# One matmul of 512 columns for two of 256 in the first half's dense products, operand tiles that stay allocated, and a three-chunk input projection

## The chip, the core and the metric

The kernel runs on one core of a Trainium2 chip. The metric is the device time of one execution in microseconds. The core has five engines that run side by side: TensorE (PE in the profile, with its weight loads as PEld), VectorE (DVE), ScalarE (ACT), GpSimd (POOL) and SyncE (SP, which only issues DMAs). TensorE's clock is granted at one of two levels, 2.4 GHz (shown as 1.0) or 1.2 GHz (0.5).

## The reference

One inference step of a trunk of two layers over T = 1088 tokens: a prompt of 1024 and eight samples of 8. All is float32. Cut to its frame:

```python
for layer in range(2):
    h = rmsnorm(x, norm_mix[layer])
    if layer == 0:
        u, q, k, v, b, a, z = split(h @ ab_w_in)          # 1024 -> 2568
        mix = concat([s5_mixer(u) with its GLU, gated_delta(q, k, v, b, a, z)]) @ ab_w_out
    else:
        r, k, v, decay, a, g = projections of h and of h shifted by a token
        y = rwkv7_scan(r, decay, k, v, a, ...)            # state 64 x 64, 16 heads, sequential in time
        mix = (norm(y) * g) @ w_o
    x = x + mix
    h = rmsnorm(x, norm_ffn[layer])
    x = x + (silu(h @ w_gate) * (h @ w_up)) @ w_down      # 1024 -> 2816 -> 1024
y = rmsnorm(x)
```

The final states of all recurrences are outputs too.

## The kernel before

Features lie on partitions (8 tiles of 128), tokens on columns. The tokens are worked in two halves (`HALF`, line 23): the first has 512 tokens in two chunks of 256, the second 576 in two chunks of 288. The order of the program is: the input projection, S5 and the first half of the gated-delta heads (`layer0`); then for each half the output projection (`project`, products `po`), the feed-forward net (`ffn`) and layer 1's projections (`RWKV.projections`, products `pj`); then for each half layer 1's output projection and feed-forward net.

A dense product (`mm`, L296) is exact to more than the matmul's own format: weight and operand are each split into a high and a low part, and for each of 8 contraction tiles there are three matmuls (high by high, high by low, low by high) into one bank of PSUM, each with its own weight load of 128 columns. A product of a whole column tile is so 24 matmuls. Each of the two chunks has its own products, one after the other, with the same weights. In the net, `pg` are the products of gate and up, `pd` those of down, which go in groups of three tiles of the hidden features (9 matmuls each). PSUM has two banks for all of these (`pa`), used in turn; VectorE empties a `pd` or `po` bank with one add into the residual stream (L508, L420), ScalarE and VectorE a `pg` bank with a tanh and products (L484 to L493). The weights come by SP's queue, are rounded on ScalarE (L284) and their low parts made on GpSimd (L285) or VectorE.

The operands' parts are tiles of one chunk each, `hi` and `lo`, taken anew for each use from rings of 16 (`hilo`, L392). The input projection (`pi`) takes all 1088 tokens in four chunks of 272 (`NCH`).

The recurrence of layer 1 (`RWKV.unit`, L1506 to L1687) goes by feature tile (8) and by segment (4 of 256 tokens, the last with the 64 sample tokens besides): 32 units. Each unit prepares its operands, inverts its triangular matrices (`inverse`, with a chain of 15 pairs of small VectorE products, L170 and L172), and then takes its 4 chunks of 64 tokens one after the other. One such step is a chain over TensorE and VectorE: L1636 (matmul into `pc`), L1638 (VectorE copy to `X`), L1640, L1642, L1644, L1647, and L1649, which leaves the state `H` for the next step. Results go to DRAM (`dyr`), and from there into layer 1's output projection. The units of the first half's segments run beside the second half's layer 0, those of the second half's segments beside the first half's layer 1.

What stands where on each engine is decided by a scheduler before the program runs: it lists the instructions by its own estimate of when each could go, and every engine then runs its list strictly in order. Nothing is moved at run time.

Of the kernel before, what the change touches and what calls it, by code (L numbers as in the profile page):

```python
# [31 lines left out]
class Fine:  # L32
    """Functions on small float32 tiles by DVE arithmetic, to float32's accuracy."""
# [42 lines left out]
    def log1p(self, out, e):  # L76
        """ln(1 + e) for e in [0, 1]."""
# [13 lines left out]
class Kern:  # L91
    def __init__(self, ctx, tc):
# [7 lines left out]
        # identity and the matrices of the norms' sums  # L100
# [14 lines left out]
        # block masks: row blocks of 16 and of 8, and which half of 32 a row is in  # L115
# [18 lines left out]
        # unit matrices of 16 in a lane's row  # L134
# [50 lines left out]
        # blocks of 32  # L185
# [24 lines left out]
        # blocks of 64  # L210
# [32 lines left out]
        # blocks of 128  # L243
# [31 lines left out]
    def weight(self, src, kt=8, m=128, tag="w", bufs=3, lo=None):  # L275
        """Loads [128, kt, m] and returns its high and low parts."""
# [67 lines left out]
    def spread(self, r):  # L344
        """stats()' result on all partitions."""
# [31 lines left out]
    def after(self, ins, n):  # L377
        """To be issued, on its engine, after the n-th of ins from their end."""
# [13 lines left out]
    def hilo(self, n=8):  # L392
        """Tiles of a chunk for the high and the low parts of n feature tiles."""
        return tuple([self.dp.tile([128, self.width], F32R, tag=t, name=t, bufs=16) for i in range(n)]
                     for t in ("hi", "lo"))
# [16 lines left out]
    def project(self, x, ys, chunks, w, ahead, n=8):  # L412
# [1650 lines left out]
```

## Time and profile before

| | us |
|---|---|
| median of 3 runs | 3808.33 (3807.59 to 3809.31) |
| the profiled execution's span | 3788.5 |
| PE busy | 3497.6 |
| DVE busy | 2510.2 |
| ACT busy | 1321.9 |
| POOL busy | 1321.9 |

The span goes from the first instruction to the last; the time of a run also has what lies around it, 19.8 us by these numbers. A busy PE is not a PE at its peak: the end of a matmul is modelled, and matmuls overlap. How long one matmul holds the engine is therefore read from how many start in a stretch in which nothing else ran, not from its mean duration.

### The profile page before, as it was taken

What the parts mean: (1) busy time and instruction counts of PE and PEld (TensorE: products, weight loads), DVE (VectorE), ACT (ScalarE), POOL (GpSimd) and SP (SyncE); (2) the same over time, 40 slices, a digit from 0 to 9 for tenths busy, and PEclk for the clock granted to TensorE, in tenths of its full rate; (3) what the DMA queues carried; (4) which work ended last, traced back from release to release, by engine and by line L of the source; (5) the groups of instructions that cost most, each with busy time, mean ns of one, the idle gap of its engine ahead of it and who ended that gap; (6) DMA issues with size and microseconds to landing.
All of it is one profiled execution on the core that took longest, in us unless ns stands there. A gap on an engine that the chain in (4) does not pass through costs nothing. (4 is left out here: it accounts for less than half of the span.)

```text
span 3788.5 us, 78549 instructions
## 1 busy us (share of the span) xinstructions
PE 3497.6 (92%) x30678; PEld 3214.4 (85%) x30678; DVE 2510.2 (66%) x6901; ACT 1321.9 (35%) x2944; POOL 1321.9 (35%) x1211
## 2 busy tenths in 40 slices
PE   7899998999988989999999889999999999899998
PEld 6889887999978877888888777888888888799997
DVE  7976878754466367777877574567788886553444
ACT  3333333222234443333333244433333333232222
POOL 3322233222235443333333264533333433332221
PEclk9989998999988999999999988998999999899999
DMA  3334442322223542122222224621222222312222
GB/s 104 93 88 124 104 126 70 93 88 95 93 73 102 184 147 70 58 78 82 87 76 73 80 73 140 210 82 54 81 88 92 90 75 82 126 64 81 88 78 69
DMA packets 331410, 356.44 MB, mean 94 GB/s; under 512 B 133272, under 2 KB 273304, under 8 KB 331040
## 3 DMA queue, kind: packets, MB, share of 16 engines
q1 hardware_dynamic: 321824, 342.52, 29.5%
q10 hardware_dynamic: 9216, 8.92, 0.7%
q8 instruction: 241, 3.95, 0.4%
q14 instruction: 129, 1.06, 0.1%
HBM read 285.34 MB, written 64.81 MB: 92 GB/s over the span
## 5 line engine op out<-in xcount | busy, mean ns | idle before, releaser
L285 POOL TENSOR_TENSOR wl<-raw,wh 128x1024 fp32r<-128x1024 f32 (+2 forms) x301 | 701.9, 2335 | 1095.7 <-ACT wh L284 1019.8
L296 PE MATMUL pg<-hi,wh 128*128 128x288 f32 (+1 forms) x2816 | 839.9, 298 | 18.8 <-DVE s L485 13.4
L296 PE MATMUL pg<-lo,wh 128*128 128x288 f32 (+1 forms) x2816 | 838.3, 298 | 6.8 <-DVE lo L383 5.0
L296 PE MATMUL pg<-hi,wl 128*128 128x288 f32 (+1 forms) x2816 | 836.8, 297 | 0.0
L296 PEld LDWEIGHTS pg<-hi,wh 128*128 128x128 f32 x2816 | 545.0, 194 | 31.3 <-DVE s L485 16.0
L296 PEld LDWEIGHTS pg<-lo,wh 128*128 128x128 f32 x2816 | 544.3, 193 | 18.1 <-DVE lo L383 7.0
L296 PEld LDWEIGHTS pg<-hi,wl 128*128 128x128 f32 x2816 | 544.7, 193 | 7.4 <-issue 1.6
L284 ACT CAST wh<-raw 128x1024 fp32r<-128x1024 f32 (+3 forms) x309 | 312.7, 1013 | 378.3 <-PE pg L296 103.9
L296 PE MATMUL pd<-ah,wdh 128*128 128x256 f32 (+1 forms) x1280 | 387.7, 303 | 20.9 <-DVE x L508 17.7
L296 PE MATMUL pd<-ah,wdl 128*128 128x256 f32 (+1 forms) x1280 | 370.7, 290 | 0.3 <-POOL wdl L285 0.3
L296 PE MATMUL pd<-al,wdh 128*128 128x256 f32 (+1 forms) x1280 | 370.7, 290 | 0.0
L296 PEld LDWEIGHTS pd<-ah,wdh 128*128 128x128 f32 x1280 | 241.9, 189 | 36.3 <-DVE x L508 21.2
L296 PE MATMUL pj<-lo,wh 128*128 128x256 f32 (+1 forms) x768 | 244.0, 318 | 17.5 <-DVE lo L383 14.5
L296 PE MATMUL pj<-hi,wh 128*128 128x256 f32 (+1 forms) x768 | 242.5, 318 | 15.7 <-ACT st L1371 7.2
L296 PEld LDWEIGHTS pd<-ah,wdl 128*128 128x128 f32 x1280 | 242.3, 189 | 1.7 <-POOL wdl L285 0.9
L296 PEld LDWEIGHTS pd<-al,wdh 128*128 128x128 f32 x1280 | 242.5, 189 | 0.8
L296 PE MATMUL pj<-hi,wl 128*128 128x256 f32 (+1 forms) x768 | 238.7, 313 | 0.4 <-POOL wl L285 0.2
L508 DVE TENSOR_TENSOR x<-x,pd 128x256 f32<-128x256 f32 (+1 forms) x384 | 162.4, 424 | 75.0 <-PE pd L296 70.7
L284 ACT CAST wdh<-raw 128x384 fp32r<-128x384 f32 (+1 forms) x224 | 111.2, 496 | 284.9 <-PE pd L296 196.8
L170 DVE TENSOR_TENSOR Tm<-L,T 32x15 f32<-32x15 f32 (+8 forms) x600 | 185.8, 310 | 29.5 <-DMA L<-dA 17.3
L172 DVE TENSOR_TENSOR T<-T,Tm 32x15 f32<-32x15 f32 (+8 forms) x600 | 184.6, 308 | 13.0
L296 PE MATMUL pi<-hi,wh 128*128 128x272 f32 x640 | 192.5, 301 | 0.2 <-ACT rows L1803 0.2
(639 smaller groups left out, 8199.9 us busy)
## 6 DMA issues: line engine op xcount, KB each, us to landing
raw<-in_wg SPq DMA_DIRECT2D x88, 512.0 KB
raw<-in_wup SPq DMA_DIRECT2D x88, 512.0 KB
raw<-in_wd SPq DMA_DIRECT2D x192, 192.0 KB
raw<-in_win SPq DMA_DIRECT2D x20, 512.0 KB
raw<-pr ACTq DMA_DIRECT2D x64, 136.0 KB
raw<-in_wk SPq DMA_DIRECT2D x16, 512.0 KB
raw<-in_wr SPq DMA_DIRECT2D x16, 512.0 KB
raw<-in_wv SPq DMA_DIRECT2D x16, 512.0 KB
```

Source lines behind the costliest of these rows:

```text
L170: v.tensor_mul(mm, L[:nl, j:j + 1, j + 1:16].to_broadcast([nl, j + 1, n]), T[:nl, 0:j + 1, j:j + 1].to_broadcast([nl, j + 1, n]))
L172: v.tensor_tensor(T[:nl, 0:j + 1, j + 1:16], T[:nl, 0:j + 1, j + 1:16], mm, op=op)
L284: nc.scalar.copy(wh, raw)
L285: (lo or nc.gpsimd).tensor_sub(wl, raw, wh)
L296: self.nc.tensor.matmul(ps, a[k], b[:, c:c + cn], start=i == 0, stop=i == last)
L508: v.tensor_add(x[m][:, c:c + cn], x[m][:, c:c + cn], ps)
```

## The change

Three things, in one diff.

1. `operands()` allocates the eight `hi` and eight `lo` tiles once, each with both chunks side by side ([128, 2, 288]); `part(i, ...)` gives the view of chunk i, `part(None, ...)` that of both as one operand of 2 x 256 columns. `hilo` and the lists of tiles that were handed around are gone.
2. In the first half (512 tokens), most dense products go over both chunks at once: one matmul of 512 columns into a whole PSUM bank where two of 256 stood. These are: gate and up of hidden tiles 2 to 21, down of all groups but the last (whose 8 output tiles still go chunk by chunk, as the norm of the next stage starts with the first chunk), in both layers; the S5 linear unit; layer 0's output projection but for its last contraction tile; tiles 0 to 5 of layer 1's output projection; keys 2 to 5, and receptances and values 1 to 5. The gate's bank is then emptied chunk by chunk (`yielded`), down's by one add of 512 columns. The second half (576 tokens, over the 512 of a bank) stays as it was.
3. The input projection takes three chunks (368, 360, 360) in place of four of 272, except for the rows and tiles that go with the norm at the very start.

```diff
+TCH = [(0, 368), (368, 360), (728, 360)]
+WIDE = 512
...
+    def operands(self):
+        self.H = tuple([self.dp.tile([128, 2, self.width], F32R, name="%s%d" % (t, k)) for k in range(8)]
+                       for t in ("hi", "lo"))
+    def part(self, i, cn, ks=range(8)):
+        return tuple([t[k][:, :, :cn] if i is None else t[k][:, i, :cn] for k in ks] for t in self.H)
...
-    def mm(self, ps, w, x, cn, c=0):
-        his, los = x
+    def mm(self, ps, w, x, cn=None, c=0):
+        his, los = x if cn is None else [[t[:, c:c + cn] for t in y] for y in x]
+        if len(his[0].shape) == 3:
+            ps = ps.rearrange("p (i c) -> p i c", i=2)
...
-                self.nc.tensor.matmul(ps, a[k], b[:, c:c + cn], start=i == 0, stop=i == last)
+                self.nc.tensor.matmul(ps, a[k], b, start=i == 0, stop=i == last)
...
         def gate(f, i, k):
+            ps = self.pa("pg")
+            if i is None:
+                self.mm(ps, fetch(f, k), self.part(None, chunks[0][1]))
+                yielded(f, 0, k, ps[:, 0:chunks[0][1]])
+                yielded(f, 1, k, ps[:, chunks[1][0]:WIDE])
+                return
...
         def gu(f):
             fetch(f, 0), fetch(f, 1)
-            for i in range(2):
+            for i in (None,) if wide else range(2):
                 for k in range(2):
                     gate(f, i, k)
...
-                    for c, cn in chunks:
+                    for c, cn in (wide,) if wide else chunks:
                         one(m, [[p[:, i] for i in range(len(G))] for p in w], c, cn)
...
+        parts = (None,) if chunks[1][0] + chunks[1][1] == WIDE else (0, 1)
+        for m in range(6 if n == 8 else 8):
             wt = self.weight(w[m][:, 0:n], n)
-            for i in range(2):
+            for i in parts:
                 one(m, wt, i)
...
-        def proj(w, put, M=128, chunks=NCH):
+        def proj(w, put, M=128, chunks=TCH):
```

With other matmuls the scheduler also lists the recurrences at other places. The first place is TensorE's list in layer 1's down products of the first half (`pd`; `pc<-XV,AR` is the first matmul of a recurrence step, `py<-H,Q` belongs to a step's output). Before:

```order
L296 MATMUL pd<-ah,wdl 128x256
L1636 MATMUL pc<-XV,AR 64x64 x2
L296 MATMUL pd<-ah,wdh 128x256
L296 MATMUL pd<-al,wdh 128x256
L296 MATMUL pd<-ah,wdl 128x256
```

After, at such a step:

```order
L311 MATMUL pd<-ah,wdl 128x512
L1664 MATMUL pc<-XV,AR 64x64 x2
L1680 MATMUL py<-H,Q 64x64
L229 MATMUL py_29570<-t_29515,MB 32x32 x10
L311 MATMUL pd<-ah,wdh 128x512
L311 MATMUL pd<-al,wdh 128x512
```

What moved is the spacing. Over the five whole groups of this net (gate, up and down of three hidden tiles each: 2160 matmuls of 256 columns before, 1080 of 512 now) the list holds 40 steps of the recurrence before and 25 after.

The second place is where that net ends on TensorE. Before, the last step of the recurrence stands among the down products of the last group but one (`pd` as above):

```order
L296 MATMUL pd<-ah,wdh 128x256
L296 MATMUL pd<-al,wdh 128x256
L296 MATMUL pd<-ah,wdl 128x256
L1636 MATMUL pc<-XV,AR 64x64 x2
L1652 MATMUL py<-H,Q 64x64
```

After, behind the net's last product, with the second half's output projection (`po`) already begun and held up by the recurrence's outputs (`pcr`, `pcs`, `pk` are the sample tokens' products):

```order
L1726 MATMUL pk<-AR,S_30929 64x16 x16
L1626 MATMUL pt<-ident,BK 128x128
L1668 MATMUL pc<-X,TT 64x64 x2
L1732 MATMUL pcr<-ident,rT 64x64 x2
L1744 MATMUL py<-ident,rT 64x128
L311 MATMUL po<-hi_5311,wh 128x288 x2
L1738 MATMUL pcs<-XV,AR 64x64 x2
L1672 MATMUL pc<-XV,BG 64x64 x2
L311 MATMUL po<-lo_5319,wh 128x288
```

Here 19 of the recurrence's 64 steps of this half stand behind the net, where none stood, and 5 in the down products of its last two groups in place of 1; among the 19 stand only some 40 dense matmuls.

The third place is VectorE's list in the two stretches. Before, beside the net (L508 empties a `pd` bank, L170 and L172 are the inversion, L1638 a step's copy):

```order
L508 TENSOR_TENSOR x<-x,pd 128x256
L170 TENSOR_TENSOR Tm<-L,T 40x60
L508 TENSOR_TENSOR x<-x,pd 128x256
L172 TENSOR_TENSOR T<-T,Tm 40x6x10
L170 TENSOR_TENSOR Tm<-L,T 40x63
L172 TENSOR_TENSOR T<-T,Tm 40x7x9
L1638 COPY X<-pc 128x64
```

After, behind the net (L1666 is the step's copy, L1675 and L1677 end a step, L1695 and L1696 are the norm of a unit's output):

```order
L1670 COPY XV<-pc 64x64
L1675 SCALAR_TENSOR_TENSOR XV<-pc,Pe,SP 64x64 x2
L1677 SCALAR_TENSOR_TENSOR H<-pc,Pe,SP 128x64
L1666 COPY X<-pc 128x64
L1670 COPY XV<-pc 64x64
L191 TENSOR_TENSOR tt<-Tc,half 128x160
L1677 SCALAR_TENSOR_TENSOR H<-pc,Pe,SP 128x64
L1695 TENSOR_REDUCE su<-py 128x4
```

Between the first half's last `pd` add and the second half's first `po` add there are now 521 VectorE instructions, nearly all of them the recurrence's. In layer 0 the heads of the gated-delta rule move the same way by one: of the five heads that stand ahead of the first feed-forward net, four now stand in the output projection's part of TensorE's list, where two stood.

## Rows read from the trace of the kernel before

**Rows 1.** The page: busy time of each engine; the granted clock in 40 slices.

```profile
PE 3497.6 (92%) x30678; PEld 3214.4 (85%) x30678; DVE 2510.2 (66%) x6901; ACT 1321.9 (35%) x2944; POOL 1321.9 (35%) x1211
...
PEclk9989998999988999999999988998999999899999
```

**Rows 2.** Windows, all engines: stretch, length, busy us and instructions, granted clock, DMA share, GB/s.

```profile
16.00:464.00 448.00, 402.67 (x3351) 371.70 (x3352) 349.14 (x970) 157.95 (x334) 116.27 (x117) 0.91 0.36 97
464.00:604.00 140.00, 131.18 (x1208) 119.06 (x1206) 111.12 (x337) 50.94 (x108) 47.39 (x44) 0.92 0.40 119
604.00:870.00 266.00, 252.31 (x2163) 237.45 (x2163) 174.87 (x547) 81.98 (x169) 77.84 (x57) 0.94 0.26 81
870.00:1060.00 190.00, 190.00 (x1602) 190.00 (x1601) 78.57 (x149) 53.88 (x96) 55.00 (x23) 1.00 0.28 92
3340.00:3730.00 390.00, 388.29 (x2917) 387.27 (x2916) 159.42 (x287) 105.80 (x185) 102.06 (x45) 1.00 0.24 79
1105.00:1380.00 275.00, 245.78 (x1635) 223.66 (x1638) 156.25 (x307) 128.40 (x298) 153.47 (x163) 0.86 0.44 138
```

**Rows 3.** Windows, dense matmuls (L296) alone: PE busy (x), PEld busy (x), granted clock.

```profile
875.00:1060.00 185.00, 185.00 (x1560) 185.00 (x1559) 1.00 0.28 89
3410.00:3730.00 320.00, 320.00 (x2410) 320.00 (x2410) 1.00 0.25 81
698.58:701.99 3.41, 3.41 (x18) 3.41 (x17) 0.50 0.41 103
```

**Rows 4.** Windows, all engines, layer 1's first half: whole, its five groups, end.

```profile
2467.00:3270.00 803.00, 741.04 (x7648) 653.85 (x7648) 618.34 (x1887) 282.94 (x710) 294.18 (x286) 0.93 0.27 86
2675.00:3158.00 483.00, 455.26 (x4784) 400.85 (x4784) 391.30 (x1215) 174.38 (x445) 180.90 (x180) 0.96 0.27 85
3254.00:3270.00 16.00, 5.56 (x82) 4.79 (x82) 12.23 (x30) 2.64 (x5) 4.75 (x2) 0.64 0.36 123
```

**Rows 5.** Windows, the recurrence's L1636 alone (four matmuls a step), columns as Rows 3.

```profile
2675.00:3158.00 483.00, 14.50 (x164) 8.67 (x164) 0.96 0.27 85
1717.00:1896.00 179.00, 5.51 (x68) 3.31 (x68) 1.00 0.26 81
2467.00:3270.00 803.00, 22.84 (x252) 13.64 (x252) 0.93 0.27 86
```

**Rows 6.** Windows, dense matmuls (L296) alone, two stretches with the recurrence beside them.

```profile
1717.00:1896.00 179.00, 132.43 (x868) 117.23 (x867) 1.00 0.26 81
2675.00:3158.00 483.00, 318.09 (x2160) 280.74 (x2160) 0.96 0.27 85
```

**Rows 7.** VectorE from 2675 to 3158 us by line: busy us, mean ns, idle before.

```profile
L172 DVE TENSOR_TENSOR T<-T,Tm 40x28 f32<-40x28 f32 (+5 forms) x153 | 55.2, 361 | 3.8
L170 DVE TENSOR_TENSOR Tm<-L,T 40x39 f32<-40x39 f32 (+9 forms) x152 | 51.9, 342 | 3.4 <-DMA L<-dA 0.2
L508 DVE TENSOR_TENSOR x<-x,pd 128x256 f32<-128x256 f32 x81 | 32.9, 409 | 4.8 <-PE pd L296 4.4
...
L493 DVE SCALAR_TENSOR_TENSOR al<-s,ah 128x256 fp32r<-128x256 f32 x30 | 13.8, 461 | 3.4 <-ACT ah L492 3.3
L485 DVE SCALAR_TENSOR_TENSOR s<-s,pg 128x256 f32<-128x256 f32 x30 | 12.3, 411 | 5.3 <-ACT s L484 5.1
L491 DVE TENSOR_TENSOR s<-s,pg 128x256 f32<-128x256 f32 x30 | 12.2, 408 | 6.6 <-PE pg L296 6.5
```

**Rows 8.** Timeline, two inversion rows: one beside a GpSimd weight split, one without.

```profile
2957.83 0.22 DVE L172 TENSOR_TENSOR T<-T,Tm 40x64 f32<-40x64 f32 x1
...
2958.35 2.39 POOL L285 TENSOR_TENSOR wl<-raw,wh 128x1024 fp32r<-128x1024 f32 x1 [3.68 <-ACT wh L284]
...
2958.55 2.26 DVE L172 TENSOR_TENSOR T<-T,Tm 40x63 f32<-40x63 f32 x1
```

More of the change, by code (lines that the diff above doesn't have):

```diff
@@ L429, in project, with project_last @@
             one(m, wt, 0)
-        steps = [lambda m=m, wt=wt: one(m, wt, 1) for m, wt in ws]
-        if n == 8:
-            return self.finish(x, chunks, steps, 6, 1, 2)
-        for f in steps:
-            f()
-    def project_last(self, x, ys, chunks, w, ahead):
+        return self.finish(x, chunks, [lambda m=m, wt=wt: one(m, wt, 1) for m, wt in ws], 6, 1, 2)
+    def project_last(self, x, chunks, w, ahead):
         ws = self.weight(w[:, :, 7].rearrange("m p c -> p m c"))
@@ L456, in ffn @@
         _, W, chunks = HALF[s]
-        hs = [self.hilo() for i in range(2)]
+        hs = [self.part(i, cn) for i, (c, cn) in enumerate(chunks)]
+        wide = (0, WIDE) if W == WIDE else None
         xc = [[t[:, c:c + cn] for t in x] for c, cn in chunks]
@@ L1292, in normed @@
                     before(t3[:, :, 1:8], h3[:, :, 0:7])
-                K.split(his[k][:, :cn], los[k][:, :cn], t, nc.gpsimd if k % 4 else v)
+                K.split(his[k], los[k], t, nc.gpsimd if k % 4 else v)
             return his, los
@@ L1364, in squares, with one, all_of @@
                 v.tensor_copy(o[:n, 2], pr[:n, 2])
-        def one(dst, m, w, h, i, kk=False):
-            c, cn = chunks[i]
-            ps = K.pa("pj")[:, :cn]
-            K.mm(ps, w, h, cn)
-            st = gp.tile([128, 288], F32, tag="st", name="st", bufs=3)[:, :cn]
-            nc.scalar.copy(st, ps)
-            nc.sync.dma_start(dst[m][:, t0 + c:t0 + c + cn], st)
-            if kk:
-                sq = K.tmp("kks")[:, :cn]
-                nc.scalar.activation(sq, ps, AF.Square, scale=self.kkc[:, m:m + 1])
-                late.append((m, i, sq))
-                if len(late) > 1:
-                    squares(*late.pop(0))
-        hs = []
+        def one(dst, m, w, i, kk=False):
+            ps = K.pa("pj")
+            both = i is None
+            K.mm(ps[:, :WIDE if i is None else chunks[i][1]], w, K.part(i, chunks[0][1]))
+            for i in range(2) if i is None else (i,):
+                c, cn = chunks[i]
+                p = ps[:, c:c + cn] if both else ps[:, :cn]
+                st = gp.tile([128, 288], F32, tag="st", name="st", bufs=3)[:, :cn]
+                nc.scalar.copy(st, p)
+                nc.sync.dma_start(dst[m][:, t0 + c:t0 + c + cn], st)
+                if kk:
+                    sq = K.tmp("kks")[:, :cn]
+                    nc.scalar.activation(sq, p, AF.Square, scale=self.kkc[:, m:m + 1])
+                    late.append((m, i, sq))
+                    if len(late) > 1:
+                        squares(*late.pop(0))
+        def all_of(dst, m, w, kk=False):
+            for i in (None,) if W == WIDE else range(2):
+                one(dst, m, w, i, kk)
         bc, r1 = norms
@@ L1392, in projections @@
         for m in range(2, 6):
-            w = K.weight(wk[m])
-            for i in range(2):
-                one(self.dk, m, w, hs[i], i, True)
+            all_of(self.dk, m, K.weight(wk[m]), True)
             lora(*loras[m - 1])
@@ L1403, in projections @@
         for j, wt, dst, more in ((0, wr, self.drr, {1: (0,), 2: (1,), 3: (2, 3), 4: (4, 5), 5: (6, 7)}), (3, wv, self.dv, {})):
-            hs = [mix(j, i) for i in range(2)]
+            for i in range(2):
+                mix(j, i)
             for m in range(6):
                 w = K.weight(wt[m])
-                for i in range(2):
-                    one(dst, m, w, hs[i], i)
+                if m:
+                    all_of(dst, m, w)
+                else:
+                    for i in range(2):
+                        one(dst, m, w, i)
                 for ft in more.get(m, ()):
@@ L1852, in mixed0 @@
     cn = 4 * kn
-    gs = [K.hilo(4) for i in range(2)]
+    gs = [K.part(i, cn, range(4, 8)) for i in range(2)]
     ys = []
@@ L1893, in loaded @@
         K.nc.sync.dma_start(t[:, :n], y[:, t0:t0 + n])
-        for (c, cn), (h, l) in zip(chunks, hs):
-            (a,), (b,) = K.hilo(1)
+        for j, (c, cn) in enumerate(chunks):
+            (a,), (b,) = K.part(j, cn, (k,))
             m = min(max(n - c, 0), cn)
@@ L1921, in trunk, with tail @@
     K.open(ctx, 288, 4, reuse_waits="tile")
-    def tail(s, src, ys, w, i, x=None, done=None, ahead=lambda: None):
+    K.operands()
+    def tail(s, src, w, i, x=None, done=None, ahead=lambda: None):
         if early is not None and s == i == 0:
@@ L1932, in gate @@
             ready[0, 0] = K.weight(I["wg"][i][0])
-        norms = K.project(x, ys, HALF[s][2], w, (lambda: None) if first else gate, 7 if first else 8)
+        norms = K.project(x, HALF[s][2], w, (lambda: None) if first else gate, 7 if first else 8)
         if first:
@@ L1937, in tail @@
             with tc.high_priority(3000):
-                norms = K.project_last(x, ys, HALF[s][2], w, gate)
+                norms = K.project_last(x, HALF[s][2], w, gate)
             second(ORDER[1])
@@ L1947, in trunk @@
         keep = lambda m, c, cn, t: nc.sync.dma_start(dx[:, m, t0 + c:t0 + c + cn], t)
-        x, norms = tail(s, I["x"], mixed0(K, s, dyg, dy, I["wglu"]), I["wout"], 0, done=keep, ahead=keys)
+        mixed0(K, s, dyg, dy, I["wglu"])
+        x, norms = tail(s, I["x"], I["wout"], 0, done=keep, ahead=keys)
         if rw is None:
@@ L1961, in trunk @@
             K.psn = rw.norm_bank
-        x, (bc, r1) = tail(s, dx, loaded(K, s, dyr, own if s else None), I["wo"], 1, rw.spare() if s else None)
+        loaded(K, s, dyr, range(8), own if s else None)
+        x, (bc, r1) = tail(s, dx, I["wo"], 1, rw.spare() if s else None)
         with tc.issue_after(K.last.ins) if s else ExitStack():
```

82 lines of the change are left out of this document (40 added, 42 removed).

## The prediction, written before the changed kernel ran

> **What bounds the kernel.** The page comes first: TensorE is busy for 92% of the span, VectorE for 66%, the others for 35% [rows 1]. A share over the span can hide stages with other limits, so the windows come next [rows 2]. Two of them are TensorE and nothing else: from 870 to 1060 us it is busy for 190.00 of 190 us at full clock, and from 3340 to 3730 for 388.29 of 390, with VectorE under 45%. Where a recurrence runs beside the products TensorE is still the fullest engine, but no longer alone: from 2675 to 3158 us it is busy for 455.26 of 483 us and VectorE for 391.30, that is 81% [rows 4]. Before 604 us VectorE has 349.14 of 448 and 111.12 of 140 us [rows 2]. So TensorE time saved is worth its full price in the pure stretches, and less where a recurrence paces the work.
>
> **What one matmul costs.** In 185 us of nothing but 256-column matmuls 1560 start: 118.6 ns each. In 320 us of 288 columns it is 2410: 132.8 ns [rows 3]. At the 2.4 GHz of these stretches 256 columns are 106.7 ns and 288 are 120.0. Beside its columns a matmul thus holds the engine some 12 ns. A matmul of 512 columns should take 213.3 + 12 = 225 ns where two of 256 take 237: **12 ns saved for each pair**. The bounds: from the difference of the two rows (14.2 ns for 32 columns, 0.444 ns each) 512 columns would be 118.6 + 256 x 0.444 = 232 ns, which saves 5; if the fixed part vanished, 24. I take 12, since the column time is the clock's. In the 1.2 GHz stretch 18 matmuls touch a window of 3.41 us, about 16 whole ones, 213 ns each [rows 3]: there the columns alone fill the time and nothing is saved.
>
> The Trainium skill (TensorE: Matmul & The Clock Gate, section Back-to-back issue gap) states a gap of N/2.4 + 2.5 ns at full clock, by which a pair would save 2.5 ns and not 12. The row of 118.6 ns stands against the 109.2 of that formula, so the row decides here.
>
> **The change, part by part.** Counted from the code, 1440 pairs become one matmul in layer 0's net (40 of 44 gate and up products of 24, and 20 of 22 hidden tiles by 8 outputs by 3 in down), as many in layer 1's net and 144 in its output projection, 168 in layer 0's output projection, 48 in the S5 unit, and 336 in layer 1's projections. The input projection drops 432 matmuls (18 column tiles of 24).
>
> - Layer 0's net: 1440 x 12 ns = 17.3 us. Half of this stage is the pure stretch; in the other part (604 to 870 us) the clock is 0.94 and TensorE busy for 252 of 266 us [rows 2]. I take **-17**.
> - Everything ahead of it: (432 + 168 + 48) x 12 = 7.8 us. VectorE is at 78 to 79% here, and a gated-delta head now stands further back in the list, behind the input projection; but the same five heads must be done before the net in both lists. Bounds 0 and -8; I take **-3**.
> - Layer 1's projections: 336 x 12 = 4.0 us at a clock of 0.86, with TensorE idle for 29 of 275 us [rows 2]: **-2.5**.
> - The kept tiles: no transfer and no arithmetic is added. A new write into a chunk's view waits for the last matmul that read that view, as a ring's slot did. What could be lost is that a wide product needs both chunks; but hidden tiles 0 and 1, and the first tile of the receptances and values, still go by chunks and cover the second chunk's preparation. Nothing. A wide `pd` bank is emptied by one add in place of two of 409 ns [rows 7], beside a product of 9 x 225 ns = 2.0 us in the other bank; a wide gate's two evacuations stand beside 5.4 us. Nothing there either.
>
> **The recurrence moves, and this is the large term.** Layer 1's first half takes 803.0 us, from 2467 to 3270 [rows 4]. In it 252/4 = 63 recurrence steps run [rows 5], beside 3552 dense matmuls (384 `po`, 2112 `pg`, 1056 `pd`). In the five whole groups, 483 us hold 2160 dense matmuls [rows 6] and 164/4 = 41 steps [rows 5]: (483 - 2160 x 0.1186)/41 = 5.53 us a step beyond the dense work. The same in layer 0's second half, where steps have no sample tokens and more dense work each: (179 - 868 x 0.1328)/17 = 3.75 us [rows 5, 6]. Between the two lies what a step costs TensorE when it seldom has to wait. So of 803 us, 421 are dense, 63 x 5.53 = 348 the steps, and 33 the rest (norms at both ends).
>
> After, the list has 44 steps up to the net's end and 19 behind it. Up to the end: dense 421 - 1584 x 0.012 = 402; 44 steps at 4.7 us (the middle, as each step now has 43 wide matmuls, 9.7 us, beside it where it had 54 x 0.1186 = 6.4 us, and so more time for its chain), 207; the rest 33 - 16, since the norm at the end [rows 4] falls into the tail; and 10 for the net's last two groups, in which 5 steps at their own pace outlast some 30 us of products. That is 636 us.
>
> **The tail** then runs with hardly a dense product to hide it. It is 521 VectorE instructions by the order. In the five groups VectorE's instructions other than the net's four kinds (71.2 us, 171 of them [rows 7]) took 391.3 - 71.2 = 320 us for 1215 - 171 = 1044 [rows 4], 0.307 us each: 521 x 0.307 = 160 us. Of this the inversion's rows would be less: they average 351 ns, but 0.22 us when no GpSimd weight split runs beside them, and 2.26 us when one does [rows 7, 8]; the tail has few splits, so some 110 of them save 0.13 us each, 14 us. VectorE's work is then 146 us. At the busy share of the five groups, 81%, the tail lasts 146/0.81 = **180 us**. Bounds: 146 (VectorE never waits) and 521 x 483/1215 = 207 (each instruction at its whole share of the shared stretch).
>
> The stretch is so 636 + 180 = 816 us against 803: **+13**, between -42 (3.75 us a step: -42; tail 146: -34; not both in full) and +79 (5.53 us: +37; tail 207: +27, and 2 more). Some 40 of the second half's `po` matmuls run inside the tail: 40 x 0.133 = **-5**.
>
> The sum against the profiled span: 3788.5 - 17 - 3 - 2.5 + 13 - 5 = 3774. The median of the runs lies 19.8 us above the span, so **3794 us**, 0.4% faster. The pairs alone promise 48 us; most of it is given back behind layer 1's first net.
>
> **The rivals.**
>
> 1. *The tail costs nothing*: VectorE alone, without TensorE's long products between its steps, runs at its full pace, 146 us, and the recurrence ends 34 us sooner: 3760. For it: many of VectorE's waits in the five groups are for TensorE (`x` for `pd`, `s` for `pg` [rows 7]), and they fall away. Against it: four links of each step's chain are on TensorE, and VectorE's list is in strict order.
> 2. *Slower: the tail keeps the shared pace*, 483/41 = 11.8 us a step: 19 x 11.8 = 224 us, 44 more than I take: 3838. For it: a step is a chain of VectorE and TensorE, units hang on one another through single buffers, and in the idle end of the stage the clock was 0.64 [rows 4], which makes the chain's matmuls longer. Against it: in the shared stretch TensorE was at 94%, which stretched the chain. It decides from a tail of 180 + 14 = 194 us on, 10.2 us a step.
> 3. *The wide matmul does not do what it says*: what a matmul has beyond its columns grows with them, 232 ns for 512 [rows 3]. The dense savings fall by 7/12 of some 42 us, 24 us: 3818. The skill's formula named above leaves still less, 2.5 of 12 ns; by it the loss would be some 33 us.
>
> **How the numbers follow.** The forecast has a chance of 0.45, rival 1 of 0.20, rival 2 of 0.25, rival 3 of 0.10. The forecast is 3794 with its own range of 3770 to 3825. About 0.2%, 7.6 us, is what a measurement of this kernel can tell from no change: faster means below 3800.7, slower above 3815.9. Of the forecast's 0.45 I put 0.27 faster, 0.10 same, 0.08 slower; rival 1 is faster (0.20); rival 2 gives 0.02, 0.03 and 0.20; rival 3 gives 0.02, 0.03 and 0.05. So 0.51 faster, 0.16 same, 0.33 slower. The range of 3752 to 3840 leaves out about one in ten on each side.
>
> **What would show it.** A pure stretch of 512-column products with some 225 ns between starts would prove the first term, with layer 0's net 17 us shorter. Behind layer 1's first net the windows should show a stretch of 150 to 220 us with VectorE at 75% or more, TensorE well under 70% and L296's successor nearly absent. If the time falls by over 40 us, the tail was cheap; if it rises, the tail is over 194 us. Wrong altogether would be a tail that isn't there, or an input projection stage longer by more than 10 us because of the head that moved back.

## The result: slower, and the profile after

The changed kernel takes 3868.89 us in the median (3856.06 to 3875.92, 4 runs) beside 3808.82 us: a ratio of 1.0158 (95% interval 1.0133 to 1.0183). Run a second time beside the kernel before (below, `after_again`) it is 1.0177 (1.0151 to 1.0203). The forecast was 3794 us with a range up to 3840: the wrong side, and outside the range.

Two lines of the page answer to [rows 1]: busy time of each engine, and the granted clock in 40 slices.

```profile
PE 3521.7 (91%) x26670; PEld 3036.6 (79%) x26670; DVE 2473.1 (64%) x6775; ACT 1317.6 (34%) x2926; POOL 1326.0 (34%) x1211
...
PEclk9989876999988899999999988999999986699999
```

TensorE issues 4008 matmuls fewer and is still busy for 24 us more. The clock slices show where the clock was lower: 876 stands in the fifth to seventh, where [rows 1] has 998, and 866 near the end, where it has 998. The mean granted clock over the span is 0.919; before it is 0.940. With two levels, 1 and 0.5, the share of time at the half clock is (1 - mean)/0.5: 16.2% of 3866.7 us is 626 us, before 12.0% of 3788.5, 455 us.

The windows, all engines, as [rows 2, 4]: the input projection, the S5 unit with the first output projection, the pure stretch of layer 0's net, layer 1's projections, layer 1's first half up to its net's end, and the stretch behind it.

```profile
14.00:438.00 424.00, 376.91 (x2659) 346.87 (x2660) 306.42 (x843) 139.83 (x284) 110.28 (x100) 0.92 0.35 96
438.00:657.00 219.00, 184.24 (x1282) 155.46 (x1280) 158.88 (x489) 70.96 (x145) 58.41 (x63) 0.77 0.36 94
...
920.00:1104.00 184.00, 184.00 (x794) 148.85 (x793) 74.37 (x147) 51.59 (x94) 55.46 (x28) 1.00 0.29 92
1149.00:1426.00 277.00, 242.81 (x1274) 200.48 (x1275) 153.18 (x299) 127.38 (x295) 152.72 (x163) 0.86 0.43 137
2524.00:3164.00 640.00, 608.08 (x4637) 464.87 (x4637) 457.00 (x1311) 232.78 (x554) 262.23 (x235) 0.97 0.29 88
3164.00:3352.00 188.00, 135.27 (x1465) 100.76 (x1466) 133.70 (x519) 48.58 (x154) 39.86 (x52) 0.59 0.24 72
```

Set against the profile before, stage by stage, by where each stage's dense products begin:

| stage | before, us | after, us | difference | forecast |
|---|---|---|---|---|
| start to layer 0's first net | 604 | 657 | +53 | -3 |
| that net | 501 | 492 | -9 | -17 |
| layer 1's projections, first half | 275 | 277 | +2 | -2.5 |
| second half's layer 0 and projections | 1087 | 1098 | +11 | 0 |
| layer 1's first half and the tail | 803 | 828 | +25 | +13 |
| to the second half's last net | 63 | 61 | -2 | -5 |
| last net and norm | 455.5 | 453.7 | -2 | 0 |

The sum is 78 us, the difference of the two spans. The medians differ by 60. After, the run of 3868.48 us has a span of 3866.7, so 1.8 us lie around a span, and not the 19.8 that the table ahead of the prediction put there; by this the profiled execution of the kernel before was quicker than the runs of its median. The +11 of the second half is no cost of the change: a second profile of the kernel before (`before_again`, below) has 1101 us there and 786 in the next row, the first had 1087 and 803, and the two sums, 1887 and 1890, agree.

Two places stand out. The second window, 219 us, is [rows 2]'s 140: four heads of the gated-delta rule run here with little beside them, at a clock of 0.77 where it was 0.92. The last window is the tail, 188 us with VectorE busy for 71% of it and TensorE at a clock of 0.59, which is 82% of the time at half clock.

Dense products alone (L311), and the recurrence's first link alone (L1664, four matmuls a step), columns as [rows 3, 5]:

```profile
925.00:1100.00 175.00, 174.71 (x752) 141.21 (x751) 1.00 0.29 94
...
2700.00:3100.00 400.00, 313.05 (x1205) 220.58 (x1206) 0.99 0.29 89
```

```profile
2524.00:3164.00 640.00, 15.24 (x176) 8.98 (x176) 0.97 0.29 88
3164.00:3352.00 188.00, 9.53 (x76) 6.41 (x76) 0.59 0.24 72
...
2700.00:3100.00 400.00, 9.38 (x108) 5.52 (x108) 0.99 0.29 89
```

A matmul of 512 columns takes 174.71/752 = 232.3 ns; a pair saves 237.2 - 232.3 = 4.9 ns. Up to the net's end run 176/4 = 44 steps, behind it 76/4 = 19, as the lists said.

### The profile page after: what moved, and what is told of

It is laid out like the page before. It is cut to its first block, busy times and chain, and to the rows that moved or that the text cites. A ratio compares the mean times of both kernels' runs of the same rounds, so it can differ in the third digit from the quotient of the medians.

```text
span 3866.7 us, 70318 instructions
## 1 busy us (share of the span) xinstructions
PE 3521.7 (91%) x26670; PEld 3036.6 (79%) x26670; DVE 2473.1 (64%) x6775; ACT 1317.6 (34%) x2926; POOL 1326.0 (34%) x1211
## 5 line engine op out<-in xcount | busy, mean ns | idle before, releaser
L311 PE MATMUL pg<-hi,wh 128*128 128x288 f32 (+2 forms) x2176 | 725.9, 334 | 26.7 <-DVE s L505 12.8
L311 PE MATMUL pg<-lo,wh 128*128 128x288 f32 (+2 forms) x2176 | 721.0, 331 | 3.2 <-POOL lo L398 1.7
L311 PE MATMUL pg<-hi,wl 128*128 128x288 f32 (+2 forms) x2176 | 721.1, 332 | 0.0
L311 PEld LDWEIGHTS pg<-hi,wh 128*128 128x128 f32 x2176 | 416.9, 192 | 64.9 <-DVE s L505 14.4
L311 PEld LDWEIGHTS pg<-lo,wh 128*128 128x128 f32 x2176 | 417.0, 192 | 37.4 <-POOL lo L398 3.1
L311 PEld LDWEIGHTS pg<-hi,wl 128*128 128x128 f32 x2176 | 417.0, 192 | 31.5 <-issue 0.9
L311 PE MATMUL pd<-ah,wdh 128*128 128x288 f32 (+1 forms) x960 | 328.2, 342 | 11.6 <-DVE x L528 7.5
L311 PE MATMUL pd<-ah,wdl 128*128 128x288 f32 (+1 forms) x960 | 321.2, 335 | 0.0
L311 PE MATMUL pd<-al,wdh 128*128 128x288 f32 (+1 forms) x960 | 318.2, 331 | 0.0
L311 PE MATMUL pj<-lo,wh 128*128 128x288 f32 (+2 forms) x656 | 225.4, 344 | 20.0 <-DVE lo L398 15.6
L311 PE MATMUL pj<-hi,wh 128*128 128x288 f32 (+2 forms) x656 | 224.7, 344 | 13.9 <-ACT hi L397 6.0
L311 PE MATMUL pj<-hi,wl 128*128 128x288 f32 (+2 forms) x656 | 220.4, 338 | 0.6 <-POOL wl L298 0.6
L311 PEld LDWEIGHTS pd<-ah,wdh 128*128 128x128 f32 x960 | 181.6, 189 | 33.6 <-DVE x L528 9.3
L528 DVE TENSOR_TENSOR x<-x,pd 128x288 f32<-128x288 f32 (+2 forms) x272 | 145.9, 540 | 84.8 <-PE pd L311 83.7
L311 PEld LDWEIGHTS pd<-ah,wdl 128*128 128x128 f32 x960 | 181.6, 189 | 16.8 <-DVE wdl L298 0.8
L311 PEld LDWEIGHTS pd<-al,wdh 128*128 128x128 f32 x960 | 182.1, 190 | 13.6
```

The costliest lines, as they stand in the source:

```text
L311: self.nc.tensor.matmul(ps, a[k], b, start=i == 0, stop=i == last)
L528: v.tensor_add(x[m][:, c:c + cn], x[m][:, c:c + cn], ps)
```

## The experiments: which part costs

The ratios are to the kernel before, run beside each. "Net" is layer 0's first net. "Stage" runs from the start of layer 1's first output projection to the start of the second half's last net (866 us in the profile before).

| kernel | input chunks | first output projection | net | layer 1's first net | ratio (95%) | net starts, us | stage, us |
|---|---|---|---|---|---|---|---|
| before_again | 4 | narrow | narrow | narrow | (one run) | 603 | 850 |
| kept_only | 4 | narrow | narrow | narrow | 1.0001 (0.9983 to 1.0018) | 612 | 840 |
| three_only | 3 | narrow | narrow | narrow | 1.0004 (0.9987 to 1.0021) | 633 | 836 |
| best_narrow | 4 | narrow | wide | narrow | 0.9969 (0.9949 to 0.9990) | 607 | 845 |
| ffn1_narrow_nch | 4 | wide | wide | narrow | 0.9970 (0.9947 to 0.9992) | 633 | 839 |
| three_po_narrow | 3 | narrow | wide | narrow | 0.9996 (0.9981 to 1.0011) | 632 | 845 |
| ffn1_narrow | 3 | wide | wide | narrow | 1.0070 (1.0048 to 1.0091) | 652 | 850 |
| four_chunks | 4 | wide | wide | wide | 1.0119 (1.0098 to 1.0139) | 631 | 894 |
| after, after_again | 3 | wide | wide | wide | 1.0158, 1.0177 | 657, 656 | 889, 889 |

The first output projection stands for the S5 unit too. From `best_narrow` on, layer 1's projections and its first output projection are wide as well.

**The chunks and the net, undone singly and together.**

```diff
-TCH = [(0, 368), (368, 360), (728, 360)]
+TCH = NCH
```

```diff
-        wide = (0, WIDE) if W == WIDE else None
+        wide = (0, WIDE) if W == WIDE and alone else None
```

The first line alone is `four_chunks`, the second alone `ffn1_narrow` (`alone` is true in layer 0's first half only), both are `ffn1_narrow_nch`.

> The changed kernel with its input projection back in four chunks of 272; all else stays, the wide products too. In TensorE's list two gated-delta heads again stand within the input projection, where the changed kernel has one. Theory A (the head that moved behind the input projection made the start longer: the first feed-forward net began at 656.7 us, before at 603.6): the first net starts within 10 us of 600 us, and the time falls from 3869 to about 3820 us. Rival B (the start is longer because the output projection's wide products wait for both chunks of their operand, so all four heads' chain is exposed): the first net still starts after 640 us and the time stays within 15 us of 3869.

> The changed kernel with the feed-forward net of layer 1's first half back in two chunks of 256; all else stays. In the list no recurrence step is left behind that net. Theory A (the tail costs more than the wide products save there): the stretch from layer 1's first output projection to its second half's net goes from 889 us back to about 866, the time to about 3845 us. Rival C (the tail was paid for by the shorter net, and the loss there is another thing, a lower clock or chance): only the 1440 pairs' saving is lost, 5.5 ns each by the changed kernel's trace, and the time rises to about 3877 us.

> Both of the edits of the two runs above at once: four chunks, and layer 1's first net by chunks; wide are only layer 0's products, layer 1's projections and its first output projection. Theory A: the two gains add, 3869 - 49 - 24 = 3796 us, which is 0.3% under the kernel before (3808). Rival (the recurrences find some other place to wait, and the gains do not add): 3815 us or more.

With both undone the change is a gain of 0.3%, or 14 us between the medians, as theory A of the third expectation has it. The loss sits in these two edits: layer 1's wide net costs 57 us with four chunks (3838.83 - 3781.70, run side by side) and 0.9 to 1.1%, 34 to 41 us, with three; three chunks cost 38 us with that net narrow (3819.88 - 3781.70), and 0.4 to 0.6%, 15 to 22 us, with it wide. The two do not add: 57 and 38 less the gain of 14 would be 81 us, and 60 to 68 are measured. Theory A and rival B of the first expectation are each half right: undoing the chunks brought the net's start from 657 to 631 us, not to 604, and 15 to 22 us of time, not 49. Of the second expectation C is out, but A's size was too small (the stage fell from 889 to 850 us, not to 866), since it was read against the profile before, whose stage was a long one:

> The kernel before itself, for a second profile of it. In the profile that the prediction used, layer 1's first half took 803 us, 710 of them from the net's start to the next output projection, with TensorE at half clock in 92 of these; kept_only, which differs in the operand tiles alone, took 776 us, with 42 at half clock in 694. If that one profile was drawn on the long side, this one shows 770 to 790 us; if the kept tiles make the stage shorter, 800 or more again.

It shows 786, the edit of the tiles alone 776 (the same window as [rows 4] first, of `before_again` and of `kept_only`):

```profile
2477.00:3263.00 786.00, 719.44 (x7648) 633.88 (x7648) 616.59 (x1887) 282.24 (x710) 295.45 (x286) 0.96 0.28 88
```

```profile
2499.00:3275.00 776.00, 719.44 (x7646) 632.13 (x7645) 612.33 (x1887) 282.85 (x710) 295.60 (x286) 0.97 0.29 89
```

The same list took 803 us at a clock of 0.93, and 786 at 0.96. The two executions may have run on different chips.

**The kept tiles**, all else as before (no wide product, four chunks):

> The changed kernel with nothing wide and four chunks: of the change only the kept operand tiles are left. If they cost nothing, as the prediction has it, 3808 us, within 8 us of the kernel before. If a kept tile's reuse makes the next product wait, some stage is longer and the time is over 3816 us. Its profile is also a second look at stages that are nearly those of the kernel before.

1.0001: they cost nothing that shows, to within 0.2%.

**What makes the start longer.** `three_only` is `kept_only` with the three chunks. `best_narrow` is `ffn1_narrow_nch` with the first two products narrow, `three_po_narrow` is that with three chunks:

```diff
-        parts = (None,) if chunks[1][0] + chunks[1][1] == WIDE else (0, 1)
+        parts = (None,) if n == 8 and chunks[1][0] + chunks[1][1] == WIDE else (0, 1)
...
-        pw = K.pa("pgl") if W == WIDE else None
+        pw = None
```

> ffn1_narrow_nch with the S5 unit's and layer 0's first output projection's products in two chunks of 256 again: wide are only layer 0's first net, layer 1's projections and its first output projection. In ffn1_narrow_nch the first net began at 633 us, in kept_only, which differs ahead of it in these products alone, at 612. If the wide products there cost those 20 us (they move the fifth head's work among the last products of the output projection), the ratio to the kernel before falls from 0.997 to 0.991 to 0.992, some 3764 us on a chip where that one takes 3796. If the 20 us were chance or return later in the net, the ratio stays at 0.995 to 0.999.

> kept_only with the input projection in three chunks: nothing is wide, one thing differs. kept_only's first net began at 612 us, four_chunks' (wide output projection, four chunks) at 631, the changed kernel's (both) at 657. If the three chunks cost by themselves (a head more stands behind the input projection in the list) the first net begins at 630 to 640 us and the ratio to the kernel before is 1.004 to 1.009. If they cost only together with the wide output projection, it begins within 8 us of 612 and the ratio is 0.997 to 1.002.

> best_narrow with the input projection in three chunks: wide are layer 0's first net, layer 1's projections and its first output projection. Measured so far, as ratios to the kernel before: four chunks with a narrow first output projection 0.997, with a wide one 0.997, three chunks with a wide one 1.007. If the three chunks cost only together with the wide S5 unit and output projection, this one is at 0.995 to 1.000. If they cost as soon as the net behind them is wide (it can no longer hide the head work that comes late), it is at 1.004 to 1.009, and its first net, begun at some 630 us, ends after 1115 us (best_narrow: 1092).

By the net's start the two delays simply add: three chunks start the net 21 to 25 us later (612 to 633, 607 to 632), the wide output projection 19 to 26 (612 to 631, 607 to 633), both 45. By time each alone is 0 to 10 us (the 0.9969 of `best_narrow` against 0.9970 and 0.9996), together 38 (1.0070); such a difference of two ratios is good to some 10 us. So `best_narrow` met its second case (the delay returns later), `three_only` the first by its net's start and the second by its time, `three_po_narrow` the first. The output projection's last contraction tile needs the fourth head's output. That head's last product on VectorE, in the kernel before, `best_narrow` (neither edit), `ffn1_narrow_nch` (wide output projection), `three_po_narrow` (three chunks), `ffn1_narrow` (both) and after (both):

```profile
550.23 1.19 DVE L1176 SCALAR_TENSOR_TENSOR OT<-zr,OT 128x512 f32<-128x512 f32 x1
```

```profile
556.13 2.48 DVE L1196 SCALAR_TENSOR_TENSOR OT<-zr,OT 128x512 f32<-128x512 f32 x1
```

```profile
567.27 0.68 DVE L1196 SCALAR_TENSOR_TENSOR OT<-zr,OT 128x512 f32<-128x512 f32 x1
```

```profile
571.54 0.69 DVE L1196 SCALAR_TENSOR_TENSOR OT<-zr,OT 128x512 f32<-128x512 f32 x1
```

```profile
599.27 0.68 DVE L1196 SCALAR_TENSOR_TENSOR OT<-zr,OT 128x512 f32<-128x512 f32 x1
```

```profile
603.51 0.69 DVE L1196 SCALAR_TENSOR_TENSOR OT<-zr,OT 128x512 f32<-128x512 f32 x1
```

Against `best_narrow` the head is 11 us late with the wide output projection alone, 15 with the three chunks alone and 43 with both. With both, that is nearly the whole delay of 45 us of the net; with one edit alone the other 10 to 15 us arise behind the head. The kernel before and the changed one take the same 53 us from this product to the net's start (550 to 604, 603.5 to 657), so all of the changed kernel's +53 arises ahead of it. The windows of the stage, in `ffn1_narrow_nch`, `three_po_narrow` and `ffn1_narrow` (both edits):

```profile
464.00:633.00 169.00, 148.68 (x1030) 122.38 (x1028) 131.25 (x396) 55.67 (x115) 48.85 (x49) 0.82 0.39 105
```

```profile
436.00:632.00 196.00, 174.44 (x1451) 156.68 (x1450) 145.87 (x459) 66.97 (x139) 57.99 (x61) 0.81 0.39 102
```

```profile
435.00:652.00 217.00, 182.19 (x1273) 153.91 (x1277) 161.80 (x488) 70.30 (x144) 59.13 (x63) 0.78 0.37 95
```

VectorE's work in the second is 146 us of 196 and in the third 162 of 217: neither engine is full, and the clock is 0.8. That the heads' chains between the two engines set the pace here is read from this; no run shows it, nor why the two edits together delay the head by more than the sum of each. Of the 26 us by which the wide output projection alone delays the net, 13 are won back in the net itself: it takes 482 us in `ffn1_narrow_nch` (633 to 1115) and 495 in `best_narrow` (607 to 1102). For the three chunks alone it stays open. The profiles of `three_only` and `kept_only` end 13 us apart and their times differ by 0.03%, but the profiled run of the first was 6.6 us over its median and that of the second 3.3 under.

**The changed kernel again**, as a common measure:

> The changed kernel itself, as the common measure for the runs beside it. Ratio 1.016 as in the result; its first net starts at 650 to 660 us, the tail lasts 180 to 200 us again if these are properties of the list and not of one execution.

The net starts at 656 us and the tail has 187: these are properties of the lists, and not of one execution.

## The experiments: where the steps stand, and the clock

**Steps back among the wide products.** Each hidden tile's products are put behind a given step; `paced_four` does it on `four_chunks`, `best_paced` on `best_narrow` with layer 1's net wide:

```diff
+            return self.tc.issue_after(self.steps[-64:][9 + 54 * f // NF].ins)
...
+                with pace(f):
```

> The changed kernel with four chunks (as the run four_chunks), and with one more thing: in layer 1's first net each hidden tile's products stand in TensorE's list behind a given step of the recurrence (step 9 + 54 f / 22 for tile f), so that the 19 steps return from behind the net into it. All products are as wide as in four_chunks, no arithmetic changes. Theory A (the loss lies in where the steps stand, not in the wide products): the tail vanishes, and against four_chunks (ratio 1.0119 to the kernel before) the time falls by some 57 us and another 1440 x 5.5 ns = 8 us below ffn1_narrow_nch: 0.995 of the kernel before. Rival D (wide products cost the steps beside them more, since a step's matmul waits for up to 232 ns each time): the net grows by what the tail loses, ratio 1.005 or more.

> best_narrow with layer 1's first net wide and paced as in paced_four. By theory A 8 us under best_narrow, ratio 0.989 to 0.990; by rival D slower than best_narrow, ratio 0.997 or more.

1.0173 (1.0142 to 1.0204) and 1.0125 (1.0102 to 1.0147): the tail was gone, and the time was no better for it. By their numbers theory A failed in both runs, and rival D was met. But TensorE's list told that the pacing was coarse. A step has three links, its groups of matmuls into `pc`; of the 57 gaps between two links, for each of the three kinds of gap, 16 to 22 held no dense matmul. So the pacing was done in threes of matmuls, on the same kernel as `best_paced`:

```diff
+            with self.paced(3 * ps.shape[-1] * (ps.shape[1] if len(ps.shape) == 3 else 1)):
...
+        k = self.links[-192:][21 + 165 * self.pace // (2 * 3168 * 256 // 2)]
+        self.pace += cols
+        return self.tc.issue_after(k.ins)
```

> As best_paced, with the pacing done finely: in layer 1's first net each three matmuls (one contraction tile) stand behind a given link of the recurrence, so that between two links of a step TensorE's list holds about 9 matmuls of 512 columns, as many columns (median 4608) as the 18 of 256 in best_narrow. In best_paced 16 to 22 of 57 such gaps were empty and others held up to 22 wide matmuls; in four_chunks the gaps were all filled, but with a median of 11 to 15 wide ones, so the net's products ran ahead of the steps. Theory E (what costs is how many columns stand between two links, not how wide they are): the net takes no longer than best_narrow's 687 us, ratio to the kernel before 0.991 to 0.997. Rival D (a link waits longer where the matmuls are wide, whatever the spacing): the net is at least 30 us longer, ratio 1.005 or more.

0.9977 (0.9964 to 0.9989), the same wide products as in `best_paced`, 56 us less. Rival D falls. Theory E comes close and isn't met to the letter: the net takes 693 us (2551 to 3244) where it allowed 687, and the ratio is 0.0007 above its range. Against the narrow `best_narrow`, 0.9969, it is no change that shows: the wide net costs nothing with this spacing, and gains nothing. Layer 1's first net up to the next output projection, in `best_paced`, `best_fine` and, narrow, `best_narrow`:

```profile
2559.00:3326.00 767.00, 668.20 (x5425) 506.04 (x5425) 555.09 (x1692) 255.86 (x649) 265.20 (x262) 0.87 0.27 80
```

```profile
2551.00:3261.00 710.00, 647.66 (x5413) 483.24 (x5410) 559.11 (x1672) 251.62 (x641) 260.22 (x258) 0.93 0.29 87
```

```profile
2557.00:3260.00 703.00, 646.79 (x6865) 568.72 (x6865) 569.96 (x1750) 257.47 (x651) 261.74 (x262) 0.96 0.30 88
```

What TensorE waits for longest in the five groups (us in total, times, longest), in `best_paced` from 2660 to 3210 us and in `best_fine` from 2660 to 3140 (`pc` and `py` are links and output of a step):

```profile
PE pc L1670 <- DVE H L1684: 17.0, 9, 4.8
PE py L1688 <- DVE XV L1677: 9.7, 6, 4.1
```

```profile
PE pc L1683 <- DVE TT L244: 7.7, 2, 5.8
PE pc L1678 <- DVE H L1694: 6.9, 6, 3.0
```

Where links stood without products between them, TensorE waited for the state `H` in stretches of up to 4.8 us, and the clock of the stage fell to 0.87, which is 199 us at the half clock where `best_fine` has 99 and `best_narrow` 56. Whether the clock, 0.93 against 0.96, is what keeps the fine version from a gain is not shown: one list alone gave 0.93 and 0.96 in two executions.

This explains the changed list too. In `best_narrow` the median gap between two links holds 4352 to 4608 columns, that is 17 to 18 products of 256, in `best_fine` 4608, 9 of 512. In `four_chunks`, where the scheduler chose, it is 11, 12 and 15 of 512 in the three kinds of gap. By these medians a wide product was listed as if it were 1.2 to 1.6 narrow ones; on the chip it is 232.3/118.6 = 1.96. So from 2700 to 3100 us 27 steps (108/4) stand beside 1205 wide products, 44.6 each, where [rows 5, 6] have 2160/41 = 52.7 narrow ones, 26.3 wide. So fewer steps were done when the net's products ran out, and the rest were left over behind them. That the spacing costs, and not the width, is what `best_fine` shows; that the scheduler's estimate made the spacing is read from these counts, and no run changed the estimate.

**The tail's clock.** Into `four_chunks`, behind each of the last 57 links (19 steps), matmuls are put that nobody reads, 8 in `four_filled`, 3 in `four_filled3`:

```diff
+        for k in K.links[-57:] if not s else ():
+            with tc.issue_after(k.ins):
+                ps = K.pa("pf")[:, :256]
+                for j in range(8):
+                    nc.tensor.matmul(ps, fill[:, 0], fill.rearrange("p a c -> p (a c)"), start=j == 0, stop=j == 7)
```

> four_chunks with work added that nobody reads: behind each of the last 57 links of the first half's recurrence (the 19 steps that stand behind layer 1's first net) stand 8 more matmuls of 256 columns, 456 in all, 54 us of TensorE at full clock. In four_chunks the stretch from that net's end to the next net has TensorE at half clock in 142 of 227 us. If the half clock is what makes the tail long, the added work keeps the clock up (half clock in under 70 us) and the stretch does not grow, or falls, for all that it computes more: ratio 1.012 or less. If the tail is the chain between TensorE and VectorE, whatever the clock, the stretch grows by some 30 to 54 us: ratio 1.020 to 1.026.

> four_filled with 3 matmuls behind each link in place of 8: 171 in all, 20 us of TensorE at full clock, 34 us less than there. In four_filled the stretch behind layer 1's first net was as long as without the added work (253 and 257 us), with less half clock. If the added matmuls lay hidden in waits that were there anyway, and the clock matters little, 3 or 8 or none are the same: ratio 1.010 to 1.012. If the added 54 us were on the path and the higher clock paid them back, then 3 of them with the clock still up give some of that as a gain: ratio 1.008 or less; if 3 don't hold the clock up, half clock is again over 120 us there and the ratio is that of four_chunks or up to 20 us more.

1.0104 (1.0087 to 1.0121) with 8, and 1.0174 (1.0142 to 1.0207) with 3; `four_chunks` had 1.0119 (1.0098 to 1.0139). From the net's end to the next net, in `four_chunks`, `four_filled` and `four_filled3` (the 227 us in the expectation start only with the output projection's first product):

```profile
3127.00:3380.00 253.00, 193.10 (x2015) 153.50 (x2013) 161.62 (x587) 65.50 (x184) 62.80 (x64) 0.69 0.24 73
```

```profile
3124.00:3381.00 257.00, 223.34 (x2471) 189.25 (x2470) 160.97 (x586) 65.73 (x184) 63.18 (x64) 0.88 0.24 73
```

```profile
3137.00:3409.00 272.00, 213.76 (x2185) 172.33 (x2184) 160.80 (x587) 64.94 (x184) 62.71 (x64) 0.75 0.23 68
```

With 3 matmuls, 20 us of them, the clock is still at half for 50% of the stretch and it grows by 19 us; with 8, 54 us of them, the clock is at 0.88 and it grows by 4. The half clock makes up (1 - 0.69)/0.5 x 253 = 157 us in `four_chunks`, 136 with 3 matmuls and 62 with 8. Between the two filled kernels, which differ in the number of added matmuls alone, 34 us more work took 15 us less time, by the ratios 0.7%: the higher clock pays for it. Against `four_chunks` a second thing differs, which weakens that comparison: there 42 of the second half's output projection matmuls run among the recurrence's steps, and in both filled kernels all of them come behind the last step. The first two rows are `four_chunks` and `four_filled`, all dense products (L311, the added ones not among them) from the net's end to the last step; the other two the rest of the stretch, all engines:

```profile
3127.00:3314.00 187.00, 16.14 (x44) 10.41 (x42) 0.62 0.24 71
3124.00:3314.00 190.00, 0.35 (x3) 0.15 (x2) 0.85 0.22 66
...
3314.00:3380.00 66.00, 54.64 (x482) 52.41 (x482) 23.82 (x62) 13.27 (x22) 20.06 (x10) 0.86 0.24 79
3313.00:3381.00 68.00, 60.91 (x542) 58.59 (x540) 26.99 (x70) 13.39 (x22) 20.11 (x10) 0.96 0.28 92
```

And the clock isn't the whole of the tail: at 0.88 the stretch is as long as it was at 0.69.

The Trainium skill (TensorE: Matmul & The Clock Gate, Terms) puts the price of throttled time at that time x (1 - K/N), here a half. By it the 95 us less of half clock from no added matmuls to 8 are worth 47; the runs have 54 us of added work less 4 us of growth, 50 paid back. From none to 3 it gives 10 us for 21, and the runs have 1; from 3 to 8 it gives 37 us for 74, and the runs have 34 + 15 = 49. So the trace agrees with the rule in size, and not to better than some 10 us.

## Why the prediction was wrong, point by point

- **What one matmul costs**: the size was wrong. 232.3 ns, not 225; 4.9 ns a pair, not 12. The upper bound of 232, drawn from the difference of the two rows in [rows 3], was exact, and with it rival 3's mechanism. The step that failed is "I take 12, since the column time is the clock's": the rows themselves said 0.444 ns a column against 0.417 at the clock, and the row of 512 columns keeps to it. Rival 3's time, 3818, was off all the same, since the loss came from elsewhere. The Trainium skill's formula (TensorE: Matmul & The Clock Gate, section Back-to-back issue gap), weighed there, gives 216 ns for 512 columns, and the page gives it for a matmul by itself, not for a stream in which each has a weight load. The row is 16 ns longer. Layer 0's net gained 9 us of 17 (it takes 492 to 495 us where it is wide behind a narrow output projection, 501 to 508 where nothing is wide).
- **Everything ahead of the net**, -3: the step that failed worst, +53. Its premise, that the same five heads must be done ahead of the net in both lists and so nothing is lost, held by the list, but it took the work for what counts, and not what stands beside it. The TensorE time saved was there: the stage behind the input projection began at 438 us, not 464. But with a head more in a stretch that has few dense products, neither TensorE (184.24 of 219 us) nor VectorE (158.88) is full, and the clock falls from 0.92 to 0.77. The text had this as its last sentence on what would be wrong altogether, with no price and no chance; its bounds of 0 and -8 had no positive end. The runs split it: the three chunks and the wide output projection are 20 to 25 us each at the net's start, and by time the one makes the other dear, 38 us with layer 1's net narrow. Why they do so stays open.
- **Kept tiles, nothing**: right to within 0.2%, 1.0001.
- **The recurrence moves**: the mechanism was right, and the size came out, in part by luck. Up to the net's end 640 us (forecast 636), 44 steps at (400 - 1205 x 0.2323)/27 = 4.45 us beyond the dense work (4.7), a tail of 188 us (180, bounds 146 and 207), VectorE at 71% (81%) with 133.70 us of work (146). The stretch is 828 us (816). The luck: with 4.9 ns a pair the dense work is 421 - 1584 x 0.0049 = 413 us and not 402, and 44 steps at 4.45 are 196 and not 207; in the tail less work at a lower share made up for each other. Rival 1, by which the tail lasts 146 us, is out; of the four links on TensorE that the text names against it a step has three. The inversion ran faster there, as said from [rows 7, 8]; by line, VectorE, in the tail:

```profile
L174 DVE TENSOR_TENSOR Tm<-L,T 40x15 f32<-40x15 f32 (+7 forms) x61 | 17.0, 278 | 6.4 <-DMA L<-dA 5.0
L176 DVE TENSOR_TENSOR T<-T,Tm 40x15 f32<-40x15 f32 (+7 forms) x61 | 13.0, 213 | 1.5
```

- **Against 803**: the base was wrong. 803 us was a long draw of this stage; other profiles of the same list or nearly the same show 786 and 776. So the stretch costs 42 to 52 us, not 13, and by time the wide net cost 57 with four chunks and 34 to 41 with three. The step that failed is the comparison with 803: the term was made against one stage of one execution, and the medians of whole runs don't show how far one stage varies.
- **Rival 2**, "the tail keeps the shared pace", was to decide from 194 us on. The tail was 188, so the mechanism of the loss was not this one, though its time, 3838, was the nearest. In its evidence it named the clock of the idle end, 0.64; the tail had 0.59, and the two filled kernels show that this clock has its price.
- **Half clock as a term**: it was in no sum. 171 us more of it (626 against 455), worth about half at most, is of the size of the whole loss, 78 us in the spans. How much of the loss the clock makes, and how much the waits that came with it, is not shown.
- **The 19.8 us on top of the span**: mis-sized. A run and its own span lie 1.8 us apart, so 18 us of the base came from setting a quick execution against the median of other runs.

## What to carry to other kernels

Where a scheduler lays out strict lists, an instruction that is made longer or shorter changes what stands beside what: count, in the new list, the dense work between two links of every chain, and give each stretch without dense work a price with a positive end, the clock included. Take the base of a stage from more than one profile, since here one stage differed by 2% (803 and 786 us) where the whole span differed by 0.1%. And take the saving of a wider matmul from the rows of two widths, here 5 ns for each pair, and not from the clock; the gain of 0.2 to 0.3% is kept where layer 1's first net, which runs beside the recurrence, is left narrow, or the spacing of its products is set by hand.

## What the runs showed of the hardware

- A matmul of these dense products, each with its own weight load, holds TensorE for 5 ns and 0.444 ns a column at the full clock: 118.6, 132.8 and 232.3 ns for 256, 288 and 512 columns. 0.417 ns a column, the 2.4 GHz clock's, with a fixed part doesn't fit the three: it leaves 11.9, 12.8 and 19.0 ns.
- Added matmuls made a stretch shorter than fewer of them did: 257 us with 456 (`four_filled`), 272 with 171 (`four_filled3`), at clocks of 0.88 and 0.75.
- One list gave a stage of 803 us at a clock of 0.93 and of 786 at 0.96 (`before`, `before_again`), so the granted clock varies between executions of the same program, which may have run on different chips.
